# Masked prefix sum at a midpoint, times a matrix: block counts by comparison, address loads of two words, a last block in three parts

## The chip, the core and the metric

The kernel runs on one core of one Trainium2 chip. The core has five engines that run their own instruction streams and meet through semaphores: PE (TensorE, matrix multiplication), DVE (VectorE), ACT (ScalarE), POOL (GpSimd) and SP (SyncE, which here only issues transfers). Transfers between the chip's main memory and the core's on-chip memory are done by 16 DMA engines. The metric is the device time of one execution in microseconds (us).

## The reference

For each of 8 sequences of 8192 rows with 512 numbers, all rows at or past `lengths[b]` are set to zero, a running sum is taken along the sequence, the running sum at row `lengths[b] // 2` is picked, and the picked row is multiplied by a 512 x 512 matrix.

```
mask = (pos < lengths[:, None, None]).astype(np.float32)
cs = np.cumsum(x * mask, axis=1)
midpoints = (lengths // 2).clip(0)
mid_features = cs[b_idx, midpoints, :]
return np.matmul(mid_features[:, None, :], w).squeeze(1)
```

Only the picked row of the running sum is used, so what has to be computed is, for each sequence, the plain sum of its first n = min(lengths // 2 + 1, lengths) rows, and then one product with `w`. In the inputs of this case n is 570, 2690, 256, 2057, 905, 3772, 3859 and 571.

## The kernel before

**Tiling.** A block is 512 rows, laid on 128 partitions with 4 rows each (1 MB). The n rows of a sequence are its whole blocks and a remainder of under 512 rows. Whole blocks are 1, 5, 0, 4, 1, 7, 7 and 1. The block that lies first in sequences 0 and 1 is loaded *blind* (tile `first`), before the lengths are known; the last whole block of sequence 7 is loaded at the end (tile `last`). The other 23 blocks, called usual, go through a ring of three buffers (`xt`), each for a pair of blocks (2 MB). The remainders go through a ring of two buffers (`rem`), cut into parts of 256, 128, 64 and fewer rows.

**The sum on PE.** A block is summed by a matrix product: 8 columns of weights, one for each sequence, pick with ones and zeros to which sequence a row belongs, and the product is added up in `s_ps` (line 491). Four such products stand side by side, 32 rows apart, one for each of the block's 4 rows per partition. At the end two copies on DVE bring `s_ps` to `s_sb` in halves (line 476), PE folds the partitions into `t_ps` with the matrix `fold` (the call at line 569), DVE transposes `t_ps` to `t_sb`, and PE multiplies by `w` into `o_ps` (line 581). The last block is not added in `s_ps`: it is added straight in `t_ps` with the weights `e_last` (`add_last`, line 557), one half of its columns of rows before the fold and one half after it. Groups of three idle matmuls (`keep_busy`, line 501) are put between the pieces of work on PE.

**Addresses.** DVE works out from the lengths how many blocks each sequence has and at which row of `x` each item of the ring begins. It does this twice: first on one partition for the first six items (`begins` and `sinces` and `addresses`, lines 382 to 390), which SP needs, and then on 128 partitions, where the weights for PE are made. The numbers n are spread to 128 partitions by a small matrix product (`n_ps`, line 518). Every instruction of DVE in this part waits for the one before it (`step`, line 329), and `s_dve` counts them: `DVE_ADDR` is the count at which the first addresses stand, `DVE_N` that at which PE may spread n, `DVE_FIRST` that at which the weights of the blind blocks stand, `DVE_MASK` that of the first remainders' weights, and `DVE_ALL` the end of the part.

**Queues.** SP issues, in this order, the lengths, the two blind blocks, the pairs of the ring and the two halves of `last`. For the ring it loads six addresses into registers (line 226, and line 232 for each further round of three pairs) and then, for each pair, waits until DVE has freed the buffer (`take` in `load`, line 204); a pair that lies in one piece is one transfer of 2 MB, another is two of 1 MB. ACT issues `w`, clears the two remainder buffers, and issues the parts of the remainders, sequence by sequence (lines 261 to 303). PE takes its work in a fixed order: the blind blocks, then in each round of the loop two sequences' remainders and three pairs, then the end. It waits for each piece by the semaphore of its buffer. DVE frees an `xt` buffer when PE is through with it and the next weights are written (line 455).

**The order** of all this is written out by hand; nothing plans it.

Of the kernel before, what the change touches and what calls it, by code (L numbers as in the profile page):

```python
# [8 lines left out]
F32 = mybir.dt.float32  # L9
# [8 lines left out]
def kernel(  # L18
# [40 lines left out]

    PARTS = [(256, 0, 2, 4), (128, 1, 4, 4), (64, 3, 4, 2)]  # L60
    WT = G * B
    xf = x.rearrange("b s d -> (b s) d")
# [12 lines left out]
    def sem(name):  # L75
        return tc.alloc_semaphore(name)
# [6 lines left out]
    lens1 = sb("lens1", [1, 2 * B], I32)  # L83
    n_i = sb("n_i", [1, B], I32)
    n_f = sb("n_f", [1, B])
    ones = sb("ones", [1, P])
    zero = sb("zero", [1, P])
    idle = sb("idle", [P, D], BF16)


# [4 lines left out]
                                      for n in ("cnt", "blocks", "has", "usual", "begin")]  # L95
    blocks1, has1, usual1, begin1 = [sb(n + "1", [1, B + (n == "begin")], I32 if n == "blocks" else F32)
                                     for n in ("blocks", "has", "usual", "begin")]
    step_c = sb("step_c", [1, B - 1])
# [35 lines left out]
    s_rdone, s_rfree, s_rem = [[sem(f"{n}{q}") for q in range(2)] for n in ("rdone", "rfree", "rem")]  # L134
    s_last = [sem(f"last{h}") for h in range(2)]
    s_first = [sem(f"first{b}") for b in range(BLIND)]
# [29 lines left out]

    DVE_SEL, DVE_ADDR, DVE_N, DVE_FIRST, DVE_MASK, DVE_ALL = 2, 22, 23, 33, 50, 59
    DVE_LAST = DVE_ALL + 6
# [26 lines left out]
    @block.sync  # L195
    def _(sp):
        hint = sp.mark_branch_hint_location()
        off, left, apart = [sp.alloc_register(f"sp_{n}") for n in ("off", "left", "apart")]
        at = [sp.alloc_register(f"sp_at{i}") for i in range(PER)]
        facts = [sp.alloc_register(f"sp_fact{i}") for i in range(2)]  # L200
        sp.reg_mov(off, BLIND + PER)

        def load(k):
            take(sp, s_free[k], 1)

            def block(h, n=1):

                to = xt[:, k].rearrange("p h g d -> p (h g) d")[:, h * G:(h + n) * G]
                sp.dma_start(
                    out=to, in_=xf[ds(sp.snap(at[2 * k + h]), n * BLK)].rearrange("(p g) d -> p g d", g=n * G)  # L210
                ).then_inc(s_full[k], 16)

            sp.reg_alu(apart, at[2 * k + 1], at[2 * k], ALU.subtract)
            with sp.If_cmp(left, 2 * k + 2, "IS_GE"):
                with sp.If_cmp(apart, BLK, "IS_EQ"):
                    block(0, 2)
                    sp.sem_inc(s_full[k], 16)
                with sp.Else():
                    block(0)
                    block(1)  # L220
            with sp.Else():
                block(0)
                sp.sem_inc(s_full[k], 16)

        sp.wait_ge(s_dve, DVE_ADDR)
        sp.load([left] + at, addr[:, BLIND - 1:BLIND + PER])
        with sp.Fori(0, rounds_of(sp, left, 1)):
            pairs(sp, left, load)
            less(sp, left, PER)
            with sp.If_cmp(left, 1, "IS_GE"):  # L230
                sp.wait_ge(s_dve, DVE_ALL)
                sp.load(at, addr[:, ds(sp.snap(off, min_val=BLIND + PER, max_val=ITEMS - PER), PER)])
                sp.reg_alu(off, off, PER, ALU.add)
                sp.reg_alu(off, off, ITEMS - PER, ALU.min)

        sp.wait_ge(s_dve, DVE_ALL)
        sp.load([facts[0]], addr[:, :1])
        sp.load([facts[1]], row_last[:])
        with sp.If_cmp(facts[0], 1, "IS_GE"):
            from_rows = xf[ds(sp.snap(facts[1]), BLK)].rearrange("(p g) d -> p g d", g=G)  # L240
            for h in range(2):
                sp.dma_start(
                    out=last[:, 2 * h:2 * h + 2], in_=from_rows[:, 2 * h:2 * h + 2]
                ).then_inc(s_last[h], 16)
        with ending(sp, "sp_last", hint):
            sp.wait_ge(s_dve, DVE_LAST)
            sp.dma_start(out=out[:, :D // 2], in_=o_sb[0][:]).then_inc(s_out, 16)
# [65 lines left out]
    @block.gpsimd  # L313
    def _(pool):
        pool.iota(item[:], pattern=[[1, ITEMS]], base=0, channel_multiplier=0)
        pool.iota(item_a[:], pattern=[[BLK, ITEMS]], base=BLK - BLIND * BLK, channel_multiplier=0)
# [8 lines left out]
    def _(dve):  # L325
# [11 lines left out]
        def shape(ap, *to):  # L337
# [4 lines left out]
        assert done == DVE_SEL  # L342
        step(dve.memset, special[:], 0.0)
        step(dve.memset, special[:, :BLIND], 1.0)
        step(dve.memset, special[:, B - 1:], 1.0)
        step(dve.memset, one8[:], 1.0)
        step(dve.memset, step_c[:], float(S))
        step(dve.memset, step_c[:, BLIND - 1:BLIND], float(S - BLK))
        dve.wait_ge(s_len1, 16)
        step(dve.tensor_scalar, out=n_i[:], in0=lens1[:, ::2], scalar1=1, scalar2=None,  # L350
             op0=ALU.logical_shift_right)
        step(dve.tensor_scalar, out=n_i[:], in0=n_i[:], scalar1=1, scalar2=None, op0=ALU.add)
        step(dve.tensor_tensor, out=n_i[:], in0=n_i[:], in1=lens1[:, ::2], op=ALU.min)

        def begins(cnt, blocks, has, usual, begin):
            parts = blocks.shape[0]
            if cnt is not None:
                step(dve.tensor_scalar, out=blocks[:], in0=cnt[:], scalar1=9, scalar2=None,
                     op0=ALU.logical_shift_right)
                step(dve.scalar_tensor_tensor, out=has[:], in0=blocks[:], scalar=1.0, in1=special[:parts],  # L360
                     op0=ALU.is_ge, op1=ALU.mult)
            if begin is None:
                return
            step(dve.tensor_tensor, out=usual[:], in0=blocks[:], in1=has[:], op=ALU.subtract)
            step(dve.tensor_tensor_scan, out=begin[:, 1:], data0=one8[:parts], data1=usual[:],
                 initial=float(BLIND), op0=ALU.mult, op1=ALU.add)

# [6 lines left out]
        def addresses(a, b):  # L374
# [6 lines left out]

        begins(n_i, blocks1, has1, usual1, begin1)
        step(dve.tensor_copy, out=addr[:, :1], in_=has1[:, B - 1:])
        step(dve.tensor_scalar, out=addr[:, 1:2], in0=begin1[:, B:], scalar1=float(-BLIND), scalar2=None, op0=ALU.add)
        step(dve.scalar_tensor_tensor, out=step_a[:], in0=usual1[:, :B - 1], scalar=float(-BLK), in1=step_c[:],
             op0=ALU.mult, op1=ALU.add)
        dve.wait_ge(s_pool, 1)
# [3 lines left out]
        step(dve.tensor_copy, out=n_f[:], in_=n_i[:])  # L391
        assert done == DVE_N, done
        step(dve.memset, since[:, :1], 1.0)
# [5 lines left out]
        dve.wait_ge(s_pe, 1)  # L399
        step(dve.tensor_copy, out=cnt[:], in_=n_ps[:, :B])  # L400
        begins(cnt, blocks, has, None, None)

        step(dve.tensor_copy, out=cur_first[:].rearrange("p k b -> p (k b)")[:, ::B + 1], in_=has[:, :BLIND])
        assert done == DVE_FIRST, done
        begins(None, blocks, has, usual, begin)
        sinces(begin, 0, ITEMS)
# [24 lines left out]
        addresses(BLIND + PER, ITEMS)  # L431
        step(dve.tensor_scalar, out=row_last[:], in0=blocks1[:, B - 1:], scalar1=BLK,
             scalar2=(B - 1) * S - BLK, op0=ALU.mult, op1=ALU.add)
# [54 lines left out]
    def _(pe):  # L488
# [28 lines left out]
        pe.wait_ge(s_dve, DVE_N)  # L517
        pe.matmul(n_ps[:, :B], lhsT=ones[:], rhs=n_f[:], start=True, stop=True).then_inc(s_pe, 1)  # L518
        pe.wait_ge(s_pool, 2)
        keep_busy()  # L520
        left, rest_rounds, has_last = [pe.alloc_register(f"pe_{n}") for n in ("left", "rests", "has")]
        pe.load([has_last, left], addr[:, :2])
        pe.reg_mov(rest_rounds, B // 2)
        rounds = rounds_of(pe, left, B // 2)
        pe.wait_ge(s_dve, DVE_FIRST)
        for b in range(BLIND):
# [30 lines left out]
        def add_last(h):  # L557
            pe.wait_ge(s_last[h], 16)
            for g in range(2 * h, 2 * h + 2):
                for j in range(4):  # L560
                    mm = add_column(j, e_last[:], last[:, g])
            return mm

        with pe.If_cmp(has_last, 1, "IS_GE"):
# [53 lines left out]
```

## Time and profile before

| | us |
|---|---|
| median of six runs | 85.65 |
| lowest and highest of the six | 84.89 and 86.55 |
| the profiled execution | 85.66 |
| its span, first to last instruction | 83.4 |

| engine | busy us | share of the span |
|---|---|---|
| PE, multiplying | 56.0 | 67% |
| PE, loading weights | 12.8 | 15% |
| DVE | 15.1 | 18% |
| ACT | 5.5 | 7% |
| POOL | 1.2 | 1% |

The transfers moved 31.25 MB, a mean of 375 GB/s over the whole span. SP's queue held 27.27 MB of it, ACT's 3.97 MB.

A profile is one execution, recorded by the hardware. Its page has busy times by engine; the span in 40 equal slices, in which a digit is the busy share in tenths (9 is 90% or more); the DMA queues; the chain of work that ended last, followed back from the end; groups of instructions; and the issues of transfers with the median time from issue to landing. The trace behind the page can be asked for stretches of time, for single lines and for the issues of a stretch. A row of the timeline gives start, length, engine, line, operation, output and inputs, shape and number of instructions. The time outside the span is 85.66 - 83.4 = 2.26 us.

### The profile page before, as it was taken

The page shows a single profiled execution, that of the slowest core. Times are in us where ns is not written, and L with a number is a line of the kernel's source. Part 1 is how long each engine was busy: PE and PEld are TensorE (multiplying, and loading weights), DVE is VectorE, ACT ScalarE, POOL GpSimd, SP SyncE. Part 2 cuts the span into 40 slices and gives each one's busy share as a digit, 9 for nine tenths or more (in the row PEclk, how much of TensorE's full clock was granted, in tenths as well). Part 3 has the DMA queues.
Part 4 walks back from the last instruction along what each step waited for, and adds up shares of the span by engine and source line. Part 5 has one row for each costly group of instructions (what it writes and reads, how often), then busy time and mean ns, then how long its engine had stood idle before and what let it go on. Part 6 is the DMA issues. An engine that isn't in the chain of part 4 may idle for free. (4 is left out here: it accounts for less than half of the span.)

```text
span 83.4 us, 1463 instructions
## 1 busy us (share of the span) xinstructions
PE 56.0 (67%) x389; PEld 12.8 (15%) x389; DVE 15.1 (18%) x80; ACT 5.5 (7%) x6; POOL 1.2 (1%) x10
## 2 busy tenths in 40 slices
PE   2739998059995199840840799989209999199730
PEld 2032011001121021110110121212002221023410
DVE  2768897000000002000000001000000000002420
ACT  2991000000000000000000000000000000000020
POOL 5000000000000000000000000000000000000000
PEclk9999999975999999999997555999985899999997
DMA  0899989999999999999999999999999999996000
GB/s 16 314 432 440 464 354 467 412 410 424 424 448 415 425 409 409 409 440 448 412 409 419 425 448 416 440 416 412 444 415 424 426 448 416 389 409 248 0 0 8
DMA packets 3394, 31.25 MB, mean 375 GB/s; under 512 B 514, under 2 KB 530, under 8 KB 1058
## 3 DMA queue, kind: packets, MB, share of 16 engines
q1 hardware_dynamic: 2466, 27.27, 77.8%
q10 hardware_dynamic: 928, 3.97, 12.0%
HBM read 31.23 MB, written 0.02 MB: 375 GB/s over the span
## 5 line engine op out<-in xcount | busy, mean ns | idle before, releaser
L491 PE MATMUL s_ps<-xt,cur 128*8 128x512 f32 x184 | 25.1, 667 | 16.4 <-PEq L142 16.4
L504 PE MATMUL idle_ps<-idle 128*128 128x512 bf16 x48 | 15.1, 428 | 0.1
L491 PE MATMUL s_ps<-rem,cur_rem 128*8 128x512 f32 x64 | 9.6, 716 | 3.3 <-PEq L142 3.3
L455 DVE TENSOR_TENSOR cur<-since 128x16 f32 x9 | 1.7, 188 | 40.6 <-DVEq L142 40.6
L491 PEld LDWEIGHTS s_ps<-xt,cur 128*8 128x8 f32 x184 | 4.2, 93 | 31.0 <-issue 31.0
L504 PEld LDWEIGHTS idle_ps<-idle 128*128 128x128 bf16 x48 | 3.6, 103 | 17.2 <-issue 14.6
L308 ACT COPY o_sb<-o_ps 8x128 f32<-8x128 f32 x2 | 0.5, 259 | 73.5 <-PE o_ps L581 73.4
L259 ACT ACTIVATE rem<-rem 128x2048 uint32<-128x2048 uint32 x2 | 3.7, 1901 | 0.0
L491 PEld LDWEIGHTS s_ps<-rem,cur_rem 128*8 128x8 f32 x64 | 1.9, 104 | 10.3 <-issue 10.3
L515 PE MATMUL s_ps<-zero 1*128 1x512 f32 x2 | 2.1, 1136 | 1.6 <-DVE zero L334 1.6
L491 PE MATMUL s_ps<-first,cur_first 128*8 128x512 f32 x16 | 2.9, 818 | 0.0
L334 DVE COPY s_sb<-s_ps 128x256 f32<-128x256 f32 x2 | 0.8, 425 | 10.2 <-PE idle_ps L508 10.2
L463 DVE COPY cur_rem<-table 128x32 f32 x6 | 1.1, 182 | 8.7 <-DVEq L142 8.7
L518 PE MATMUL n_ps<-n_f,ones 1*128 1x8 f32 x2 | 0.6, 367 | 1.8 <-DVE n_f L334 1.8
L259 ACT ACT_TABLE_LOAD x1 | 1.3, 1283 | 1.4 <-PEq L602 1.4
L581 PE MATMUL o_ps<-wt,t_sb 128*8 128x128 f32 x32 | 1.1, 273 | 0.4 <-DVE t_sb L334 0.4
L497 PE MATMUL t_ps<-last,e_last 128*8 128x128 f32 x32 | 1.3, 272 | 0.0
L334 DVE TENSOR_TENSOR part_a<-since,step_a 1x42 f32<-1x42 f32 (+1 forms) x2 | 1.1, 574 | 0.1
L518 PEld LDWEIGHTS n_ps<-n_f,ones 1*128 1x128 f32 x2 | 0.5, 306 | 3.4 <-DVE n_f L334 3.4
L497 PE MATMUL t_ps<-s_sb,fold 128*8 128x128 f32 x8 | 0.8, 274 | 0.2
L581 PEld LDWEIGHTS o_ps<-wt,t_sb 128*8 128x8 f32 x32 | 0.8, 89 | 0.7 <-issue 0.7
L334 DVE TENSOR_TENSOR since<-item,begin 1x42 f32<-1x42 int32 (+1 forms) x2 | 0.8, 424 | 0.1
(64 smaller groups left out, 13.2 us busy)
## 6 DMA issues: line engine op xcount, KB each, us to landing
xt<-in_x_dram SPq DMA_DIRECT2D x10, 2048.0 KB, 13.1
xt<-in_x_dram SPq DMA_DIRECT2D x3, 1024.0 KB, 9.1
first<-in_x_dram SPq DMA_DIRECT2D x2, 1024.0 KB, 7.9
rem<-in_x_dram ACTq DMA_DIRECT2D x3, 512.0 KB, 8.7
wt<-in_w_dram ACTq DMA_DIRECT2D x1, 1024.0 KB, 4.7
last<-in_x_dram SPq DMA_DIRECT2D x2, 512.0 KB, 7.3
rem<-in_x_dram ACTq DMA_DIRECT2D x3, 256.0 KB, 9.2
rem<-in_x_dram ACTq DMA_DIRECT2D x3, 128.0 KB, 8.6
```

The costliest lines, as they stand in the source:

```text
L259: act.memzero(rem[:, q]).then_inc(s_rfree[q], 1)
L308: copy = act.copy(out=o_sb[1][:, j * P:(j + 1) * P], in_=o_ps[64 + 32 * j:64 + 32 * j + B, :P])
L334: do(*args, **kw).then_inc(s_dve, 1)
L455: dve.tensor_tensor(out=cur[:, k], in0=since[:, :B, here].rearrange("p b h -> p h b"), in1=since[:, 1:, here].rearrange("p b h -> p h b"), ...
L463: dve.tensor_copy(out=cur_rem[:, q], in_=rests[:, ds(dve.snap(of, min_val=1, max_val=B // 2 - 1), 1), q].rearrange("p o w -> p (o w)"),).t ...
L491: return pe.matmul(s_ps[32 * j:32 * j + B], lhsT=weights, rhs=rows, start=False, stop=False, skip_group_check=True, tile_position=(0, 32 * j))
L497: return pe.matmul(t_ps[32 * j:32 * j + B, :P], lhsT=weights, rhs=row[:, P * j:P * (j + 1)], start=False, stop=False, skip_group_check=Tru ...
L504: pe.matmul(idle_ps[:], lhsT=idle[:, :P], rhs=idle[:], start=True, stop=True)
L515: pe.matmul(s_ps[:], lhsT=zero[:], rhs=zero[:, :1].to_broadcast((1, D)), start=True, stop=False, skip_group_check=True)
L518: pe.matmul(n_ps[:, :B], lhsT=ones[:], rhs=n_f[:], start=True, stop=True).then_inc(s_pe, 1)
L581: mm = pe.matmul(o_ps[32 * j:32 * j + B, :P], lhsT=t_sb[:, kc, :B], rhs=wt[:, kc, j * P:(j + 1) * P], start=(kc == 0), stop=(kc == KC - 1) ...
```

## The change

There are four edits.

1. *Counting.* The number of usual blocks of a sequence was worked out from its length by a shift, an addition, a minimum, a shift, a comparison and a subtraction. Now POOL writes a table `steps` with 8 thresholds for each sequence, and DVE compares the length with all of them (`above`) and adds up how many it reaches.
2. *Address loads.* SP loads the count and two addresses instead of six, and two further addresses after each pair that it has issued. The wait for `DVE_ALL` moves into the third pair of a round.
3. *Spreading.* PE spreads the lengths themselves to 128 partitions, sooner in DVE's order, and n is worked out there. The fact whether there is a last block is written later, and PE loads its two registers after the wait for `DVE_FIRST` instead of before it.
4. *Last block.* The last block comes in three transfers of 256, 128 and 128 rows instead of two of 256. PE adds the first ahead of the fold, the second between the two halves of the fold, and the third after it. One branch holds all of it, with the fold repeated in the other branch.

```diff
+    CUTS = [0, 2, 3, 4]
...
-    DVE_SEL, DVE_ADDR, DVE_N, DVE_FIRST, DVE_MASK, DVE_ALL = 2, 22, 23, 33, 50, 59
+    DVE_SEL, DVE_ADDR, DVE_N, DVE_FIRST, DVE_MASK, DVE_ALL = 2, 15, 6, 32, 49, 58
...
-            sp.reg_alu(apart, at[2 * k + 1], at[2 * k], ALU.subtract)
+            sp.reg_alu(apart, at[1], at[0], ALU.subtract)
...
+            if k == NS - 1:
+                sp.wait_ge(s_dve, DVE_ALL)
+            sp.load(at, addr[:, ds(sp.snap(off, min_val=BLIND + 2, max_val=ITEMS - 2), 2)])
+            sp.reg_alu(off, off, 2, ALU.add)
+            sp.reg_alu(off, off, ITEMS - 2, ALU.min)
 
         sp.wait_ge(s_dve, DVE_ADDR)
-        sp.load([left] + at, addr[:, BLIND - 1:BLIND + PER])
+        sp.load([left] + at, addr[:, BLIND - 1:BLIND + 2])
         with sp.Fori(0, rounds_of(sp, left, 1)):
             pairs(sp, left, load)
             less(sp, left, PER)
-            with sp.If_cmp(left, 1, "IS_GE"):
-                sp.wait_ge(s_dve, DVE_ALL)
-                sp.load(at, addr[:, ds(sp.snap(off, min_val=BLIND + PER, max_val=ITEMS - PER), PER)])
...
-            for h in range(2):
-                sp.dma_start(
-                    out=last[:, 2 * h:2 * h + 2], in_=from_rows[:, 2 * h:2 * h + 2]
-                ).then_inc(s_last[h], 16)
+            for h, (a, b) in enumerate(zip(CUTS, CUTS[1:])):
+                sp.dma_start(out=last[:, a:b], in_=from_rows[:, a:b]).then_inc(s_last[h], 16)
...
+        for a, b, one in ((0, BLIND, 2), (BLIND, B - 1, 1), (B - 1, B, 2)):
+            pool.iota(steps[:, a:b], pattern=[[0, b - a], [2 * BLK, K]], base=one * 2 * BLK - 2,
+                      channel_multiplier=0)
...
-        step(dve.tensor_scalar, out=n_i[:], in0=lens1[:, ::2], scalar1=1, scalar2=None,
-             op0=ALU.logical_shift_right)
-        step(dve.tensor_scalar, out=n_i[:], in0=n_i[:], scalar1=1, scalar2=None, op0=ALU.add)
-        step(dve.tensor_tensor, out=n_i[:], in0=n_i[:], in1=lens1[:, ::2], op=ALU.min)
+        step(dve.tensor_copy, out=len_f[:], in_=lens1[:, ::2])
...
-        begins(n_i, blocks1, has1, usual1, begin1)
-        step(dve.tensor_copy, out=addr[:, :1], in_=has1[:, B - 1:])
+        dve.wait_ge(s_pool, 1)
+        step(dve.tensor_tensor, out=above[:], in0=shape(lens1[:, ::2].unsqueeze(2), 1, B, K), in1=steps[:],
+             op=ALU.is_ge)
+        step(dve.tensor_reduce, out=usual1[:], in_=above[:], axis=mybir.AxisListType.X, op=ALU.add)
+        step(dve.tensor_tensor_scan, out=begin1[:, 1:], data0=one8[:1], data1=usual1[:],
+             initial=float(BLIND), op0=ALU.mult, op1=ALU.add)
...
-        step(dve.tensor_copy, out=cnt[:], in_=n_ps[:, :B])
+        step(dve.tensor_copy, out=len_i[:], in_=n_ps[:, :B])
+        step(dve.tensor_scalar, out=cnt[:], in0=len_i[:], scalar1=1, scalar2=None, op0=ALU.logical_shift_right)
+        step(dve.tensor_scalar, out=cnt[:], in0=cnt[:], scalar1=1, scalar2=None, op0=ALU.add)
+        step(dve.tensor_tensor, out=cnt[:], in0=cnt[:], in1=len_i[:], op=ALU.min)
...
-        pe.matmul(n_ps[:, :B], lhsT=ones[:], rhs=n_f[:], start=True, stop=True).then_inc(s_pe, 1)
+        pe.matmul(n_ps[:, :B], lhsT=ones[:], rhs=len_f[:], start=True, stop=True).then_inc(s_pe, 1)
...
+        pe.wait_ge(s_dve, DVE_FIRST)
         pe.load([has_last, left], addr[:, :2])
...
-        pe.wait_ge(s_dve, DVE_FIRST)
...
         with pe.If_cmp(has_last, 1, "IS_GE"):
             add_last(0)
-        for j in range(4):
-            if j % 2 == 0:
-                pe.wait_ge(s_dve, DVE_ALL + 1 + j // 2)
-            mm = add_column(j, fold[:], s_sb)
-        with pe.If_cmp(has_last, 1, "IS_GE"):
-            mm = add_last(1)
-            mm.then_inc(s_pe, 1)
+            fold_half(0)
+            add_last(1)
+            fold_half(1)
+            add_last(2).then_inc(s_pe, 1)
         with pe.Else():
-            tell()
+            fold_half(0)
+            fold_half(1).then_inc(s_pe, 1)
```

The three memsets of `special` move from ahead of the lengths to behind the first addresses.

More of the change, by code (lines that the diff above doesn't have):

```diff
@@ L83 @@
     lens1 = sb("lens1", [1, 2 * B], I32)
-    n_i = sb("n_i", [1, B], I32)
-    n_f = sb("n_f", [1, B])
+    len_f = sb("len_f", [1, B])
+    len_i = sb("len_i", [P, B], I32)
     ones = sb("ones", [1, P])
@@ L95 @@
                                       for n in ("cnt", "blocks", "has", "usual", "begin")]
-    blocks1, has1, usual1, begin1 = [sb(n + "1", [1, B + (n == "begin")], I32 if n == "blocks" else F32)
-                                     for n in ("blocks", "has", "usual", "begin")]
+    K = S // 2 // BLK
+    steps = sb("steps", [1, B, K], I32)
+    above = sb("above", [1, B, K])
+    usual1, begin1 = [sb(n + "1", [1, B + (n == "begin")]) for n in ("usual", "begin")]
     step_c = sb("step_c", [1, B - 1])
@@ L134 @@
     s_rdone, s_rfree, s_rem = [[sem(f"{n}{q}") for q in range(2)] for n in ("rdone", "rfree", "rem")]
-    s_last = [sem(f"last{h}") for h in range(2)]
+    s_last = [sem(f"last{h}") for h in range(len(CUTS) - 1)]
     s_first = [sem(f"first{b}") for b in range(BLIND)]
@@ L198, in _ @@
         off, left, apart = [sp.alloc_register(f"sp_{n}") for n in ("off", "left", "apart")]
-        at = [sp.alloc_register(f"sp_at{i}") for i in range(PER)]
+        at = [sp.alloc_register(f"sp_at{i}") for i in range(2)]
         facts = [sp.alloc_register(f"sp_fact{i}") for i in range(2)]
-        sp.reg_mov(off, BLIND + PER)
+        sp.reg_mov(off, BLIND + 2)
         def load(k):
@@ L209, in block @@
                 sp.dma_start(
-                    out=to, in_=xf[ds(sp.snap(at[2 * k + h]), n * BLK)].rearrange("(p g) d -> p g d", g=n * G)
+                    out=to, in_=xf[ds(sp.snap(at[h]), n * BLK)].rearrange("(p g) d -> p g d", g=n * G)
                 ).then_inc(s_full[k], 16)
-            sp.reg_alu(apart, at[2 * k + 1], at[2 * k], ALU.subtract)
+            sp.reg_alu(apart, at[1], at[0], ALU.subtract)
             with sp.If_cmp(left, 2 * k + 2, "IS_GE"):
@@ L229, in _ @@
             less(sp, left, PER)
-            with sp.If_cmp(left, 1, "IS_GE"):
-                sp.wait_ge(s_dve, DVE_ALL)
-                sp.load(at, addr[:, ds(sp.snap(off, min_val=BLIND + PER, max_val=ITEMS - PER), PER)])
-                sp.reg_alu(off, off, PER, ALU.add)
-                sp.reg_alu(off, off, ITEMS - PER, ALU.min)
         sp.wait_ge(s_dve, DVE_ALL)
@@ L342, in _ @@
         assert done == DVE_SEL
-        step(dve.memset, special[:], 0.0)
-        step(dve.memset, special[:, :BLIND], 1.0)
-        step(dve.memset, special[:, B - 1:], 1.0)
         step(dve.memset, one8[:], 1.0)
@@ L349, in _ @@
         dve.wait_ge(s_len1, 16)
-        step(dve.tensor_scalar, out=n_i[:], in0=lens1[:, ::2], scalar1=1, scalar2=None,
-             op0=ALU.logical_shift_right)
-        step(dve.tensor_scalar, out=n_i[:], in0=n_i[:], scalar1=1, scalar2=None, op0=ALU.add)
-        step(dve.tensor_tensor, out=n_i[:], in0=n_i[:], in1=lens1[:, ::2], op=ALU.min)
[L355 to L366, printed above, removed]
+        step(dve.tensor_copy, out=len_f[:], in_=lens1[:, ::2])
+        assert done == DVE_N, done
         def sinces(begin, a, b):
@@ L386, in _ @@
              op0=ALU.mult, op1=ALU.add)
-        dve.wait_ge(s_pool, 1)
         sinces(begin1, BLIND, BLIND + PER)
@@ L390, in _ @@
         assert done == DVE_ADDR, done
-        step(dve.tensor_copy, out=n_f[:], in_=n_i[:])
-        assert done == DVE_N, done
+        step(dve.memset, special[:], 0.0)
+        step(dve.memset, special[:, :BLIND], 1.0)
+        step(dve.memset, special[:, B - 1:], 1.0)
         step(dve.memset, since[:, :1], 1.0)
@@ L399, in _ @@
         dve.wait_ge(s_pe, 1)
-        step(dve.tensor_copy, out=cnt[:], in_=n_ps[:, :B])
-        begins(cnt, blocks, has, None, None)
+        step(dve.tensor_copy, out=len_i[:], in_=n_ps[:, :B])
+        step(dve.tensor_scalar, out=cnt[:], in0=len_i[:], scalar1=1, scalar2=None, op0=ALU.logical_shift_right)
+        step(dve.tensor_scalar, out=cnt[:], in0=cnt[:], scalar1=1, scalar2=None, op0=ALU.add)
+        step(dve.tensor_tensor, out=cnt[:], in0=cnt[:], in1=len_i[:], op=ALU.min)
+        step(dve.tensor_scalar, out=blocks[:], in0=cnt[:], scalar1=9, scalar2=None, op0=ALU.logical_shift_right)
+        step(dve.scalar_tensor_tensor, out=has[:], in0=blocks[:], scalar=1.0, in1=special[:],
+             op0=ALU.is_ge, op1=ALU.mult)
         step(dve.tensor_copy, out=cur_first[:].rearrange("p k b -> p (k b)")[:, ::B + 1], in_=has[:, :BLIND])
+        step(dve.tensor_copy, out=addr[:, :1], in_=has[:1, B - 1:])
         assert done == DVE_FIRST, done
-        begins(None, blocks, has, usual, begin)
+        step(dve.tensor_tensor, out=usual[:], in0=blocks[:], in1=has[:], op=ALU.subtract)
+        step(dve.tensor_tensor_scan, out=begin[:, 1:], data0=one8[:], data1=usual[:],
+             initial=float(BLIND), op0=ALU.mult, op1=ALU.add)
         sinces(begin, 0, ITEMS)
@@ L431, in _ @@
         addresses(BLIND + PER, ITEMS)
-        step(dve.tensor_scalar, out=row_last[:], in0=blocks1[:, B - 1:], scalar1=BLK,
+        step(dve.tensor_scalar, out=row_last[:], in0=blocks[:1, B - 1:], scalar1=BLK,
              scalar2=(B - 1) * S - BLK, op0=ALU.mult, op1=ALU.add)
@@ L558, in add_last @@
             pe.wait_ge(s_last[h], 16)
-            for g in range(2 * h, 2 * h + 2):
+            for g in range(CUTS[h], CUTS[h + 1]):
                 for j in range(4):
@@ L562, in add_last, with fold_half @@
             return mm
+        def fold_half(h):
+            pe.wait_ge(s_dve, DVE_ALL + 1 + h)
+            for j in range(2 * h, 2 * h + 2):
+                mm = add_column(j, fold[:], s_sb)
+            return mm
         with pe.If_cmp(has_last, 1, "IS_GE"):
             add_last(0)
-        for j in range(4):
-            if j % 2 == 0:
-                pe.wait_ge(s_dve, DVE_ALL + 1 + j // 2)
-            mm = add_column(j, fold[:], s_sb)
-        with pe.If_cmp(has_last, 1, "IS_GE"):
-            mm = add_last(1)
-            mm.then_inc(s_pe, 1)
+            fold_half(0)
+            add_last(1)
+            fold_half(1)
+            add_last(2).then_inc(s_pe, 1)
         with pe.Else():
-            tell()
+            fold_half(0)
+            fold_half(1).then_inc(s_pe, 1)
         with ending(pe, "product", hint):
```

## The prediction

> **What bounds the kernel now.** I read the slices of the span first.
>
> ```profile
> PE   2739998059995199840840799989209999199730
> ...
> PEclk9999999975999999999997555999985899999997
> DMA  0899989999999999999999999999999999996000
> GB/s 16 314 432 440 464 354 467 412 410 424 424 448 415 425 409 409 409 440 448 412 409 419 425 448 416 440 416 412 444 415 424 426 448 416 389 409 248 0 0 8
> ```
>
> Each slice is 83.4 / 40 = 2.085 us. The DMA row stands at 8 or 9 from the second slice to the 36th, at about 423 GB/s, while PE has holes (0, 1, 2) in the middle. 31.25 MB at 0.423 MB/us is 73.9 us; the transfers run from about 2.5 to 76.6 us. So the stream is the bound, and only two stretches lie outside it: 2.5 us before it and 6.8 us after it. The change leaves the bytes alone.
>
> Next, the chain that ended last, in order of time (start, length, what):
>
> ```profile
> 72.56 0.21 issue
> 72.78 1.90 PE s_ps L491 x16
> ...
> 75.49 1.04 PE s_ps L491 x8
> 76.54 0.08 PE idle_ps L508
> ...
> 77.10 0.43 DVE s_sb L334
> ...
> 77.58 0.85 PE t_ps L497 x20
> ```
>
> It begins at 72.56, where the last full pair has landed, and then runs PE, DVE (two copies of `s_sb`), PE without a wait for data. The timeline of that place splits the last row:
>
> ```profile
> 76.36 0.62 PE L497 MATMUL t_ps<-last,e_last 128*8 128x128 f32 x16
> ...
> 77.12 0.85 PE L497 MATMUL t_ps<-s_sb,fold 128*8 128x128 f32 x8
> ...
> 77.71 0.70 PE L497 MATMUL t_ps<-last,e_last 128*8 128x128 f32 x16
> ```
>
> Eight operations appear as 16 records. The first half of the last block is multiplied while DVE copies, the second only after the fold. Last, the DMA issues of the stretches round 69.3, 9.0, 11.2 and 7.9 us, with time from issue to landing, and SyncE's register loads (minimum/median/maximum in ns):
>
> ```profile
> last<-in_x_dram SPq DMA_DIRECT2D x1, 512.0 KB, 6.9
> ...
> last<-in_x_dram SPq DMA_DIRECT2D x2, 512.0 KB, 7.3
> ...
> rem<-in_x_dram ACTq DMA_DIRECT2D x1, 256.0 KB, 7.4
> ...
> rem<-in_x_dram ACTq DMA_DIRECT2D x1, 32.0 KB, 6.3
> ...
> xt<-in_x_dram SPq DMA_DIRECT2D x1, 2048.0 KB, 9.3
> ...
> L226 SPq TENSOR_LOAD <-addr x1: 1676/1676/1676, 5.2 to 5.2; - x1
> ...
> L232 SPq TENSOR_LOAD <-addr x3: 726/754/1281, 14.5 to 52.2; - x3
> ```
>
> The first half of `last`, issued at 69.31, lands at 76.21. The second (two with median 7.3, so 7.6), issued about 69.85, lands at 77.45. The 1.24 us between is 0.524 MB at 423 GB/s: the landings follow the stream, a fixed lag behind its bytes.
>
> **Head: counting blocks and two addresses.** On DVE, from the landing of the lengths to the first addresses, 14 dependent steps start between 2.38 and 5.03, so (5.03 - 2.38) / 13 = 0.204 us a step, done at 5.18. After the change there are 10. Three memsets of `special` (0.32 us together) also leave the front; ACT's first load of the lengths starts at 2.2, so the chain starts there rather than at 2.06. The comparison has 64 elements; the nearest row, `part_a` with 42, took 0.21, so I add 0.1. Addresses stand at 2.2 + 10 x 0.204 + 0.1 = 4.3: 0.85 us sooner. The new iotas on POOL (three, 0.12 to 0.18 each by the old ones) push its last iota from 1.58 to about 2.0, ahead of the comparison at 2.4.
>
> SyncE's load of seven words took 1.68 us; it becomes three. A one-word load took 0.29, PE's two-word load 0.73; I take 0.73, bounds 0.3 and 1.0. From load end to the first `xt` issue were 7.94 - 6.88 = 1.06 us. New first issue: 4.3 + 0.73 + 1.06 = 6.1 instead of 7.94. The second and third follow 1.4 us apart as before, plus a two-word load with its arithmetic, about 0.8: near 8.3 and 10.5, against 9.40 and 10.78.
>
> What is 1.8 us worth? The first bytes of the program came 1.2 us after their issue (1.27 to about 2.5), so today's `xt` can start near 9.2. The two blind blocks and `w`, 3.15 MB, are through only at 10.0 by the sum of the half-microsecond stretches, which move 423 GB/s from 3 to 10 and 419 from 10 to 12.5. There is no hole to fill; the cover is the second blind block, landing at 10.6. I value the head at nothing. Without that cover it would be worth the full 1.8 us.
>
> In the loop the new load stands behind the issue on SP, so it runs while SP waits for a free buffer (36.1 us in nine waits). Its wait for the complete address table in the first round delays only the fourth pair, which waits until 23.89 anyway, against a table ready at 14.4. After the last pair one load more stands ahead of `last`: issue near 70 instead of 69.31. The bytes of `last` can move only after the last single, landing at 75.0; with the lag of 1.3 us between landing and bytes that is 73.6, so 1.2 us of start leave 2.4 us.
>
> **Lengths spread as they are.** The matmul that spreads them is released after 6 DVE steps instead of 23, but the conversion on 128 partitions adds three steps, and `special` three. `DVE_FIRST` is the 32nd step instead of the 33rd; it moves from 7.45 to about 7.3. PE now loads its two registers behind it: 0.73 us, then three idle matmuls of 0.43. The first blind block starts at about 9.5 instead of 8.9, and queued behind it are the second and the first remainder. PE then has nothing until 17.49, when the second remainder lands; before, it stood idle from 14.3. Cover 3 us, cost zero. If the pause on PE also left it at the slow early rate (1.9 us for a blind block against 1.04), it would arrive at 17.8, and even 0.5 us there is less than the 2.2 us of slack below.
>
> **Last block in three parts.** The half after the fold shrinks from 16 records to 8. Fifteen starts took 0.70 - 0.27 = 0.43 us, 0.029 each, so 8 fewer are 0.23 us off the path. The middle part goes between the folds: fold records end near 77.25, eight more at 77.48, the second copy is ready at 77.53; nothing added. What is late next is the third part's landing. It has the same last byte, so 77.45, against its use at 77.71: 0.26 us to spare. The Trainium skill speaks against this cut ("DMA: Bandwidth & Descriptors", "Anatomy of one DMA" and "Bandwidth"): some 2.0 us fixed a transfer plus bytes at 436 GB/s (a fit for DMAs issued by GpSimd), and batches of a MiB or more. If fixed parts added up, a further transfer would cost 2 us, and the sum would be 85.66 - 0.23 + 2.0 - 0.26 = 87.2. The row says otherwise: two halves 1.24 us apart leave no room for 2.0 us between them. I follow the row. Packets fall from 4 KB to 2 KB in the last half; from 16 KB to 4 KB the rate fell from about 426 to 401 at full share, 6%. I take 6% more on 0.524 MB, +0.08; bounds 0 and +0.3, of which 0.26 is covered.
>
> **Sum.** The profiled execution took 85.66 us (span 83.4 and 2.26 around it), as the median of the six runs, 85.65. 85.66 - 0.23 = 85.43.
>
> **The rivals.** *The early stream stumbles, and the earlier issue mends it* (faster). For it: from the landing of the second blind block (10.6) to that of the first pair (7.94 + 9.3 = 17.24) are 6.64 us; the bytes between, the pair and the 128, 256 and 32 KB remainders, are 2.52 MB, 5.96 us at 423 GB/s. The slices dip to 354. Against it: the next slice has 467, and the sum of bytes shows no loss. If the 0.68 us are lost and come back: 85.43 - 0.68 = 84.75.
>
> *The earlier pairs push the second remainder back* (slower). PE takes the second remainder before the first pair, and its release starts the fourth pair. The 256 and 32 KB transfers of it are issued by ACT at 9.03 and 11.19; the second pair moves from behind the first of these to ahead of it. The Trainium skill's "DMA: Bandwidth & Descriptors" ("Queues, rings and completion order") has each DMA engine take turns between queues packet by packet: 32 KB would then pass in about two packets of 16 KB (0.6 us each) and the lag. It took 6.3 us, so much already queued does go ahead. But it landed 0.25 us after the first pair, though two further pairs (landing 22.7 and 28.6) had been issued before it: what went ahead was that pair, no more. By the rule the delay is zero, by strict order of issue a whole pair: landing with the second pair, 22.7 instead of 17.49, 5.2 us later. The slack: the third pair's bytes end at 28.58 - 1.3 = 27.3, the fourth needs 1.2 us to start, so it may be issued at 26.1 instead of 23.89, 2.2 us. Beyond that the stream runs dry: 5.2 - 2.2 = 3.0, so 85.43 + 3.0 = 88.4. It decides from a delay of 2.2 us.
>
> *The third part lands late*: 0.5 us beyond its cover, by completion of small transfers, gives 85.9.
>
> **How the numbers follow.** A measurement of this kernel tells about 1% (0.86 us) from no change. Tail only, 85.4: 0.52, nearly all of it within 1% (0.43), with the runs' own scatter of 84.89 to 86.55 giving 0.05 faster and 0.04 slower. Mended stream, 84.75, on the bound itself: 0.30, 0.24 faster and 0.06 same. Remainder pushed back: 0.12, 0.10 slower, 0.02 same. Late third part: 0.06, 0.04 same, 0.02 slower. Sums: faster 0.29, same 0.55, slower 0.16. The range runs from somewhat below the mended stream, 84.5, to the late third part with scatter, 86.2; the pushed remainder is left out.
>
> **What would show it.** First `xt` issue near 6.1; DMA row unbroken and its end within 0.3 us of 76.6; second remainder used at 17.5, fourth pair issued before 26; after the second copy of `s_sb` 4 fold and 8 `last` records, transposes starting 0.23 us closer to the copies. Wrong if: the stream ends over 0.5 us earlier or has a dip about 24 to 30 us, or PE waits between the second fold and the third part.

## The result, and the profile after

The changed kernel takes 84.54 us (median of 36 runs, 84.33 to 88.07) against 85.46 for the kernel before (73 runs); the ratio is 0.9913, 95% interval 0.9897 to 0.9930. That is 0.74 us less (0.87% of 85.46). Single executions of either kernel are slower than the rest, and the ratio leaves them out, so it is not the quotient of the two medians (0.989). The forecast of 85.43 from 85.66 was a ratio of 0.9973: the direction and the range (84.5 to 86.2) hold, the size does not. Only a third of the gain was foreseen as the likeliest case. The time lies nearer to where the first rival put it (84.75 from 85.66, a ratio of 0.989); the range holds because its lower end came from that rival, and by little.

The profiled execution of the changed kernel took 84.88 us with a span of 83.1, so it is one of its longer ones. Outside its span lie 84.88 - 83.1 = 1.78 us, against 2.26 in the profiled execution before. Most executions of both kernels have about 1.8 there, so of the 0.78 us between the two profiled times some 0.5 are not a gain of the change. Its slices:

```profile
PE   2950799639998397830792799937408999399720
...
PEclk9999999996599999999559759999998589999999
DMA  2799999999999999999999999999999999998000
GB/s 32 296 434 410 469 422 434 405 443 418 414 438 425 388 450 387 418 422 454 433 399 426 420 420 434 418 438 414 427 426 441 426 418 434 394 402 308 0 1 7
```

The picture is that of before: a stream at about 423 GB/s without a visible gap. What has gone is the fall in the sixth slice (354 before, 422 now). A slice alone proves little: a further trace with the head of before (the first experiment below) reads 424, 424 and 398 in the fifth to seventh slice. The chain that ended last, in order of time:

```profile
72.39 0.21 issue
72.61 1.90 PE s_ps L492 x16
...
76.38 0.08 PE idle_ps L509
...
76.48 0.43 DVE s_sb L340
...
76.96 1.09 PE t_ps L498 x24
...
78.08 0.26 DVE t_sb L340
```

It starts 0.17 us sooner, because the last pair landed sooner, and DVE begins the transposes at 78.08 where it began them at 78.45. The rows of the end in the timeline, first two of the kernel before, then the changed kernel's:

```profile
76.64 0.88 DVE L334 COPY s_sb<-s_ps 128x256 f32<-128x256 f32 x2 [10.16 <-PE idle_ps L508]
...
78.45 0.53 DVE L334 STREAM_TRANSPOSE t_sb<-t_ps 128x64 f32<-128x64 f32 x2 [0.93 <-PE t_ps L497]
```

```profile
76.48 0.88 DVE L340 COPY s_sb<-s_ps 128x256 f32<-128x256 f32 x2 [10.70 <-PE idle_ps L509]
...
77.42 0.28 PE L498 MATMUL t_ps<-s_sb,fold 128*8 128x128 f32 x2
...
77.55 0.48 PE L498 MATMUL t_ps<-last,e_last 128*8 128x128 f32 x6
78.08 0.53 DVE L340 STREAM_TRANSPOSE t_sb<-t_ps 128x64 f32<-128x64 f32 x2 [0.71 <-PE t_ps L498]
```

From the end of the second copy (76.48 + 0.88 = 77.36) to the transposes are 0.72 us; before they were 78.45 - 77.52 = 0.93. The issues of transfers (the stretches round 6.4, 9.0, 11.2, 69 and 70 us) and SP's first register load:

```profile
xt<-in_x_dram SPq DMA_DIRECT2D x1, 2048.0 KB, 10.5
...
rem<-in_x_dram ACTq DMA_DIRECT2D x1, 256.0 KB, 7.7
...
rem<-in_x_dram ACTq DMA_DIRECT2D x1, 32.0 KB, 6.7
...
last<-in_x_dram SPq DMA_DIRECT2D x1, 512.0 KB, 7.2
...
last<-in_x_dram SPq DMA_DIRECT2D x1, 256.0 KB, 7.4
...
L235 SPq TENSOR_LOAD <-addr x1: 864/864/864, 4.5 to 4.5; - x1
```

The first pair is issued at 6.36 and lands at 16.86 (6.36 + 10.5); before, it was issued at 7.94 and landed at 17.24. (The view gives the time to landing to a tenth.) In both traces the same transfers had landed by then, the 128 and the 256 KB remainder among them, and the 32 KB one had not. So the same transfers were through 0.38 us sooner, although the second blind block had landed 0.16 us later. That is the first sign that the early issue closes something.

### The profile page after: what moved, and what is told of

Same layout as the page of the kernel before. It is cut to its first block, busy times and chain, and to the rows that moved or that the text cites. A ratio compares the mean times of both kernels' runs of the same rounds, so it can differ in the third digit from the quotient of the medians.

```text
span 83.1 us, 1486 instructions
## 1 busy us (share of the span) xinstructions
PE 56.9 (68%) x389; PEld 13.3 (16%) x389; DVE 15.2 (18%) x79; ACT 5.5 (7%) x6; POOL 1.6 (2%) x13
## 5 line engine op out<-in xcount | busy, mean ns | idle before, releaser
L492 PE MATMUL s_ps<-xt,cur 128*8 128x512 f32 x184 | 26.8, 705 | 14.7 <-PEq L146 14.7
L498 PEld LDWEIGHTS t_ps<-last,e_last 128*8 128x8 f32 x32 | 1.0, 89 | 0.3 <-issue 0.3
L519 PEld LDWEIGHTS n_ps<-len_f,ones 1*128 1x128 f32 x2 | 0.7, 332 | 1.0 <-DVE len_f L340 0.5
## 6 DMA issues: line engine op xcount, KB each, us to landing
xt<-in_x_dram SPq DMA_DIRECT2D x10, 2048.0 KB, 12.5
```

The lines of the kernel that those rows point to most:

```text
L492: return pe.matmul(s_ps[32 * j:32 * j + B], lhsT=weights, rhs=rows, start=False, stop=False, skip_group_check=True, tile_position=(0, 32 * j))
L498: return pe.matmul(t_ps[32 * j:32 * j + B, :P], lhsT=weights, rhs=row[:, P * j:P * (j + 1)], start=False, stop=False, skip_group_check=Tru ...
L519: pe.matmul(n_ps[:, :B], lhsT=ones[:], rhs=len_f[:], start=True, stop=True).then_inc(s_pe, 1)
```

## The experiments

Two theories were set against each other. *The tail*: only the end gains, 0.23 us, and the rest is something else. *The early stream*: behind the blind blocks the stream has a hole, which the earlier issue closes.

**The end alone.** The kernel before, with the fourth edit:

```diff
+    CUTS = [0, 2, 3, 4]
...
-            for h in range(2):
+            for h, (a, b) in enumerate(zip(CUTS, CUTS[1:])):
```

and PE's end as in the changed kernel.

> The kernel before with the fourth edit alone (last block in three parts). Theory of the tail: all of the gain that has a place in the trace is here, 8 matmul records less behind the second copy, 0.23 us, ratio to before 0.997; the rest of the measured gain (0.87% in all) would then stay unexplained. Theory of the early stream: the same 0.23 us, and the other 0.5 us are missing here. If the cut also costs landing time, this is above 0.997. If the tail is worth more than its records, because its length also varies from run to run, it is below 0.995.

Measured: ratio 0.9967 (0.9936 to 0.9998), 0.28 us. The end was priced rightly. The traces show it more sharply than the times: the idle time of DVE ahead of the transposes, the last figure of the two rows above, is 0.93 us in the trace of before and in the three experiments below that have the last block in two halves, and 0.71 in all the others.

**All but the end.** The changed kernel with the last block in two halves again:

```diff
-    CUTS = [0, 2, 3, 4]
+    CUTS = [0, 2, 4]
```

and PE's end as in the kernel before.

> The changed kernel with its fourth edit undone (last block in two halves). Theory of the tail: 1.000 to before, since the stream of transfers has no hole that an earlier issue could fill. Theory of the early stream: the first pair, issued 1.6 us earlier, takes 0.5 us off (0.994), and the spread of the runs is as narrow as with the whole change.

Measured: 0.9945 (0.9912 to 0.9978), 0.47 us. In its trace the first pair, issued at 6.35, lands at 16.95. The two parts multiply to 0.9967 x 0.9945 = 0.9912, the measured whole; with intervals of 0.003 to either side, that they agree to the last digit is chance. So the head, which was valued at nothing, brings nearly two thirds (0.19 to 0.75 us by its interval).

**A delay that was none.** Two kernels put one and two spare loads of six words ahead of SP's first load:

```diff
         sp.wait_ge(s_dve, DVE_ADDR)
+        for _ in range(1):
+            sp.load(spare, addr[:, BLIND:BLIND + 6])
         sp.load([left] + at, addr[:, BLIND - 1:BLIND + 2])
```

> The changed kernel with one spare load of six address words on SP ahead of the first, which puts the first pair's issue back to about 7.7 us, where the kernel before had it. Theory of the tail: as the changed kernel, 0.991 to before, or at least no different from it. Theory of the early stream: the 0.5 us are lost again, 0.997, and the runs scatter as before.

> As the last, with two spare loads: first issue at 8.5 to 9 us. Theory of the tail: still no loss, since the blind blocks cover the queue until 10.0 us and a transfer starts 1.2 us after its issue, so up to 8.8 is free. Theory of the early stream: worse than one spare load by the further delay, up to 1 us, 1.005.

Measured: 0.9928 (0.9900 to 0.9957) and 0.9932 (0.9898 to 0.9966). This reads like a verdict against the early stream, and is none: nobody reads the spare registers, and the built program does not have the loads. The trace of the second has one load, of 863 ns, and the first issue at 6.35; that of the first has one load too, of 889 ns. The two are repetitions of the changed kernel, beside the same runs of the kernel before as the two above.

**A delay that holds.** SP waits for a later step of DVE, with nothing else touched. This is the edit for step 24; two more kernels have 32 and 20 in its place:

```diff
-        sp.wait_ge(s_dve, DVE_ADDR)
+        sp.wait_ge(s_dve, 24)
```

> The changed kernel with one number changed: SP waits for the 24th step of DVE instead of the 15th before it loads its first addresses, so that the first pair is issued at about 7.95 us, as in the kernel before; all else as in the changed kernel. (The two spare loads of the earlier trial were left out of the built program because nothing read their registers, so that trial only repeated the changed kernel: first issue at 6.35 in the trace.) Theory of the early stream: the first pair lands at 17.2 instead of 16.8, 0.3 to 0.4 us of the gain are lost, ratio to before 0.996. Theory that another part of the head gains (the order of work on PE, the lengths spread early): no loss, 0.992, and the first pair lands at 16.8.

> As the last with a wait for the 32nd step: first issue at about 9.6 us. Theory of the early stream: the queue of SP runs dry at 10.0 while the first bytes come at 10.8, so at least 0.8 us more are lost than with the 24th step, 1.005 or above. If the place of the issue costs nothing before the stream is dry, the loss against the changed kernel is 0.8 us alone, 1.001.

> The changed kernel with SP waiting for the 20th step of DVE: first issue at about 7.15 us, between the changed kernel's 6.36 and the 7.94 of the kernel before. If the loss has a threshold, as a queue that is refilled in time or not, there is no loss yet: 0.992 to the kernel before, since the kernel with two-word loads alone has its issue there and gains all that the head gains. If the loss is in proportion to the delay, half of it is there: 0.994.

Measured, with the first issue and the landing of the first pair from the traces:

| kernel | first issue, us | landing, us | ratio to before | 95% interval |
|---|---|---|---|---|
| changed, wait for step 15 | 6.36 | 16.86 | 0.9913 | 0.9897 to 0.9930 |
| step 20 | 7.14 | 16.74 | 0.9946 | 0.9894 to 0.9997 |
| step 24 | 7.94 | 17.04 | 0.9969 | 0.9917 to 1.0020 |
| step 32 | 9.60 | 18.30 | 0.9997 | 0.9968 to 1.0026 |

With the issue put back to where it was before (step 24), the ratio is what the end gives alone (0.9967), but its interval overlaps the changed kernel's, so this run by itself decides nothing. Step 32 does: its interval is clear of the changed kernel's, and the order of work on PE and the lengths spread early are the same in both. So a first issue as late as 9.60 costs the head's gain; that an earlier issue is enough to bring it is shown by the short loads alone, below. Step 32 was expected at 1.005 by the theory of the early stream, 0.8 us above step 24; that was missed, for the times are 0.28% or 0.24 us apart, within their noise. One line of each trace shows the change, the first pair's time from issue to landing with step 24 and with step 32:

```profile
xt<-in_x_dram SPq DMA_DIRECT2D x1, 2048.0 KB, 9.1
```

```profile
xt<-in_x_dram SPq DMA_DIRECT2D x1, 2048.0 KB, 8.7
```

In these two executions an issue 1.66 us later shortens the way to the landing by only 0.4, so 1.26 us of that delay reach the stream. That this is more than the 0.24 us of the times has to do with which executions were traced: step 24's took 84.77 us, one of its shortest (84.64 to 88.75), step 32's 85.95, its longest.

Whether the loss begins at a threshold between 6.4 and 7.9 or grows in proportion, the interval of step 20 doesn't tell: its runs lie from 84.29 to 84.53 and from 85.28 on, with none between. Its one trace, of 84.51 us, shows no loss. Taken together the traces speak for a threshold. From the landing of the second blind block to that of the first pair they have 6.0, 6.1 and 6.3 us with the issue at 7.13 to 7.15, no more than the 6.1 to 6.2 at 6.35 (6.4 in the one without idle work, below); with the issue at 7.94 or 7.95 they have 6.4 to 6.6, and 7.6 at 9.60. One trace does not fit: that of the kernel with one spare load, an execution of 86.94 us, has 7.1 with the issue at 7.21.

**Two words at a time, alone and with the end.** The kernel before with the second edit, and with the second and the fourth. In both SP has the short loads:

```diff
-        sp.load([left] + at, addr[:, BLIND - 1:BLIND + PER])
+        sp.load([left] + at, addr[:, BLIND - 1:BLIND + 2])
```

> The kernel before with the second edit alone: SP loads three words instead of seven, and two after each pair; the counting, the spreading and the last block as before. First issue at about 7.1 us, since the load took 0.86 us instead of 1.68 in the traces. Theory of the early stream: half of the head's gain, ratio 0.997. Theory of another part of the head: 1.000.

> The kernel before with the second and the fourth edit, without the comparison and without the spreading. Theory of the early stream: these two carry the whole gain, 0.9955 x 0.9967 = 0.992. If the comparison and the spreading gain by themselves, it stays above 0.995.

Measured: 0.9955 (0.9915 to 0.9995), which holds the 0.997 expected, and 0.9868 (0.9800 to 0.9935, six runs, median 84.57). The first issue is at 7.15 and 7.13. The second edit, with its load of three words instead of seven, already brings what the whole head brings, within the intervals, with the order of work on PE and the spreading as before; the comparison, which moves the issue on to 6.36, and the spreading add nothing that these runs can tell.

**The hole measured by filling it.** If a hole lies behind the blind blocks, a further transfer put there costs less than its bytes. Both kernels got one of 512 KB (its tile and the wait for it at the very end are not shown):

```diff
+    nc.sync.dma_start(
+        out=pad[:], in_=xf[2 * S:2 * S + 2 * P].rearrange("(p g) d -> p g d", g=2)
+    ).then_inc(s_pad, 16)
```

> The kernel before with one transfer more, 512 KB into a tile that nobody reads, issued by SP right behind the two blind blocks: it lengthens the cover of the first pair's issue by 0.524 MB, 1.24 us at 423 GB/s. If the stream has a hole behind the blind blocks that the early issue closes, the transfer fills it: the time rises by 1.24 less the hole of 0.5, 0.7 us, ratio to the kernel before 1.009. If there is no such hole, it rises by 1.24 us, 1.0145.

> The changed kernel with the same transfer of 512 KB behind the blind blocks. Its hole is closed, so the whole 1.24 us are paid: 0.991 + 0.0145, 1.0055 to the kernel before, and the gain over the kernel before with the same transfer is only that of the end, 0.3 us. If the early issue gains in another way than by the hole, the gap between the two stays at 0.75 us and this one is at 1.000 or the other at 1.0145.

Measured: 1.0073 (1.0037 to 1.0109) for the kernel before and 1.0032 (1.0002 to 1.0062) for the changed one. The transfer costs 1.24 us of stream at 423 GB/s. The kernel before pays 0.73% of 85.42, 0.62 us, so some 0.6 us of it (0.3 to 0.9 by the interval) fill a hole. The changed kernel pays 1.0032 - 0.9913 = 1.19%, 1.02 us: nearly the whole, within the noise. The first pair's time from issue to landing, the kernel before first:

```profile
xt<-in_x_dram SPq DMA_DIRECT2D x1, 2048.0 KB, 10.1
```

```profile
xt<-in_x_dram SPq DMA_DIRECT2D x1, 2048.0 KB, 11.8
```

So it lands at 7.94 + 10.1 = 18.0 and 6.35 + 11.8 = 18.2. The transfer puts the landing back by 0.8 us in the kernel before (17.24 without it) and by 1.3 in the changed one (16.86), there by the whole of its bytes. The heads of the chain in both, the kernel before first:

```profile
73.39 0.27 issue
73.67 1.90 PE s_ps L496 x16
```

```profile
73.45 0.22 issue
73.67 1.90 PE s_ps L497 x16
```

With the longer cover the last pair is taken at the same time in both, 73.67, though the first pairs were issued 1.6 us apart (7.94 and 6.35). What is left between their times, 0.41% or 0.35 us, is about the end's share, though with both intervals at 0.3% and more this difference alone could not tell it from 0.75. What decides is the cost in the kernel before: the early stream's 1.009 lies in the interval, and the tail's 1.0145 outside it.

**The idle work on the chain.** The changed kernel without the three idle matmuls ahead of the last single, 0.75 us on the chain:

```diff
-                keep_busy()
+                if k < NS - 1:
+                    keep_busy()
                 take(pe, s_full[k], 32)
```

> The changed kernel without the three idle matmuls ahead of the third pair of each round, which stand on the chain at the end (0.75 us between the last full pair and the last single). The single has landed 0.3 to 0.5 us before PE takes it, so up to 0.5 us come off the chain there; then the third part of the last block, landing 0.18 us before its use, ends last: 0.2 us gained in all, 0.989 to the kernel before. If PE's clock falls for lack of the idle work, it is slower than the changed kernel.

Measured: median 84.46, ratio 0.9857 (0.9797 to 0.9916, seven runs); the kernel with the second and fourth edits had 0.9868 beside the same runs, so no gain over the changed kernel is shown, and the interval, which holds the 0.989 expected, excludes none. Its chain starts later:

```profile
75.13 0.44 issue
75.56 1.04 PE s_ps L492 x8
```

The single landed at 75.02, and PE began it at 75.56, 0.54 after; in the changed kernel it landed at 74.79 and was begun at 75.34, 0.55 after. What lies between is on PE's instruction stream in both: the wait passes some 0.03 us after the landing, and the branch that tells a single from a pair (line 545, with this edit 546) is recorded at 0.22 to 0.25 us after it and takes 0.23. The idle matmuls only fill a time in which PE would not have started. The expectation of 0.5 us on the chain took the row of the chain for its cost.

## Why the prediction was right or wrong

**The bound and the end: right.** The stream sets the time, and everything moves with it. The 8 records behind the second copy, 0.029 us each, were to bring 0.23 us; the trace has 0.93 - 0.72 = 0.21 and the runs 0.28. The middle part lies between the folds without cost. The three parts land at 76.13, 76.75 and 77.37, 0.62 us apart, which is 0.262 MB at 423 GB/s: the fixed 2 us a transfer of the Trainium skill ("DMA: Bandwidth & Descriptors", "Anatomy of one DMA") do not add up here, as the row of before said. But the third part's cover shrank to 0.06 us (landed at 77.37, first used at 77.43) from the 0.26 that was reckoned. The use at 77.71, on which that rested, stood 0.19 us behind the end of the second copy (77.52), with four fold records ahead of it; now the first use stands 0.07 behind it (77.36), among them.

**The head: wrong, in one step.** The issue at 6.1 was nearly met (6.36; the load took 0.86, not 0.73, and the addresses stood at 4.42, not 4.3), and so were the next two (8.54 and 10.63 against 8.3 and 10.5). The step that failed is the one behind it: "There is no hole to fill; the cover is the second blind block." It rested on the sum of bytes in half-microsecond stretches, 419 GB/s from 10 to 12.5. In quarters the same trace of the kernel before reads (stretch and its length; us busy and instructions of each engine; PE's clock, DMA share, GB/s):

```profile
10.25:10.50 0.25, 0.25 (x4) 0.00 (x0) 0.21 (x2) 0.00 (x0) 0.00 (x0) 1.00 2.96 934
10.50:10.75 0.25, 0.25 (x5) 0.03 (x2) 0.22 (x2) 0.00 (x0) 0.00 (x0) 1.00 0.50 197
10.75:11.00 0.25, 0.25 (x6) 0.13 (x3) 0.20 (x2) 0.00 (x0) 0.00 (x0) 1.00 0.76 328
11.00:11.25 0.25, 0.25 (x3) 0.07 (x1) 0.22 (x1) 0.00 (x0) 0.00 (x0) 1.00 0.77 328
11.25:11.50 0.25, 0.25 (x3) 0.01 (x2) 0.19 (x1) 0.00 (x0) 0.00 (x0) 1.00 0.77 328
```

Three quarters in a row have about 0.77 of the engines busy, and one ahead of them reads 934 GB/s at a share of 2.96, twice the rate of the fastest slice (467). That quarter lifted the mean back to 419, and with it the hole disappeared from the sum. The packets of the trace tell what it is. They are counted whole in the stretch in which they start, and 12 of the first pair's first 16 packets, of 16 KB each, start in this quarter: 197 of its 234 KB. Each takes 0.61 us or more, so most of these bytes belong to later quarters. For the same reason a low quarter is no hole yet; the changed kernel's trace has one as well, and makes it up in the next:

```profile
10.50:10.75 0.25, 0.25 (x4) 0.00 (x0) 0.21 (x2) 0.00 (x0) 0.00 (x0) 1.00 0.37 156
10.75:11.00 0.25, 0.25 (x4) 0.00 (x0) 0.18 (x3) 0.00 (x0) 0.00 (x0) 1.00 1.35 573
```

With the bytes of each packet spread over its own time, the stretch from 10 to 12.5 us reads 391 GB/s in the kernel before and 426 in the changed one; the difference is 0.09 MB, 0.2 us. The other traces go with the first issue: 389 and 404 at 7.95 and 7.94, 331 at 9.60, 417 to 429 at 6.35 to 7.15, and 421 with the further transfer in either kernel. (The exception is again the execution of 86.94 us, 376 at 7.21.) The engines are busy all the same, at a mean share of 1.00 to 1.02 in these traces. So the hole is not a pause: in the kernel before the pair's first 16 packets took 0.61 to 1.34 us each, with the issue at 7.13 to 7.15 all took 0.61, and with the further transfer 0.61 to 0.67.

The other reading, landing to landing, stood in the prediction as the first rival: 0.68 us missing between the second blind block and the first pair. (Its bytes had the 32 KB remainder in them, which landed after the pair; without it 0.75 are missing, and in the changed kernel's trace 0.2.) It was given 0.30; the runs put the head at 0.47 us and the hole at about 0.6, each with some 0.3 to either side.

The second part of that step, a start 1.2 us after the issue, was too short as well. It was the time to the first bytes of the program; the full rate came only near 3.0 us, over 1.7 after the issues at 0.88 and 1.27. With step 32, where the blind blocks leave nothing ahead of it, the pair's first packet starts at 11.13, 1.5 us after its issue.

**The other rivals.** The remainder was pushed back, but by little: the 32 KB part lands at 17.89 instead of 17.49. That is nearer to the nothing of queues that take turns than to the 5.2 us of strict order, and 0.4 us of the 2.2 of slack; the fourth pair goes out at 24.41. The second remainder was used at 18.05, not at the 17.5 forecast, and no dip follows. The third part did not land late. The steps on PE slipped more than reckoned (first blind block at 10.27, not 9.5, `DVE_FIRST` at 7.66, not 7.3) without cost, as the cover of 3 us held.

**What stays open.** Why the pair's first packets are slow, and the stream with them, when the pair is issued at 7.94 and not at 7.15, although packets of the blind blocks still start at 9.86. Nor is it shown why the runs have a larger loss than the 0.2 us that the packets of this stretch lack; 0.2 lies at the lower end of the head's interval. Lengths that land late would put the issue back in some executions, which would fit the wide scatter of the kernel before (84.80 to 87.30). They did land late in one trace, of the kernel with one spare load: DVE's first step on them begins at 3.10 instead of 2.10, and the first pair is issued at 7.21. That execution took 86.94 us, more than this delay explains, and in the one trace of the kernel before the lengths landed in time.

## What to carry to other kernels

Whether a stream has a hole is read from landings and the bytes between them, or packet by packet. A view that counts a packet whole where it starts can hide a hole behind a burst when its stretches are no longer than a packet (0.61 us here). A transfer of known size put into the suspected place measures the hole directly: what it costs less than its bytes is the hole. And a delay for an experiment must be something that the built program keeps: a wait for a later step does, a load into registers that nobody reads does not.

## What was not expected of the hardware

SP's first register load took 0.86 us with three words and 1.68 with seven. It is not a price by the word alone: the later loads of six words in the kernel before took 0.73 to 1.28, and the later ones of two words in the changed kernel 0.47 to 0.49. Ahead of the first issue of a stream, the edit that shortened the load was worth 0.45% by itself (0.05% to 0.85%). The DMA engines can be busy throughout while the stream is slow: the first packets of a 2 MB load took up to 1.34 us instead of 0.61 when it was issued at 7.94. And PE began the last single about 0.55 us after it had landed, with or without idle matmuls in front of it.
